# Attention of a two-block kernel's second mixer, computed by pairs of heads instead of head by head

## The chip, the cores and the metric

The kernel runs on one core of a Trainium2 chip. The core has a matrix engine (TensorE, PE in the profile, with its weight loads shown apart as PEld), a vector engine (VectorE, DVE), a scalar engine (ScalarE, ACT), GpSimd (POOL), and SyncE (SP), whose queue issues the transfers from the device's main memory. Each engine works through its own list of instructions in order; they meet through semaphores. SBUF is the on-chip memory, PSUM the accumulators into which TensorE writes; both have 128 partitions. The metric is the device time of one execution in microseconds (us).

## The reference, cut to what matters

Two transformer blocks of two layers each run one after the other on 256 tokens of width 1024. The second block's layer has a modulated norm, a mixer, and a gated feed-forward. Its mixer has three attention branches over the same 256 tokens, whose outputs are multiplied by branch weights, gated and summed:

```python
o_na = neighborhood_attention(qa, ka, va, na_rpb)        # 4 heads of 64, bias and window mask
o_mla = blocked_attention(q_full, k_full, v_b, 96**-0.5) # 4 heads, keys of 96, values of 64
o_gqa = blocked_attention(q_c, k_c, v_c, 64**-0.5)       # 8 query heads of 64 on 2 key/value heads
merged = (sigmoid(ga) * (o_na @ w_br_na) + sigmoid(gb) * (o_mla @ w_br_mla)
          + sigmoid(gc) * (o_gqa @ w_br_gqa))
x = x + g_m * (merged @ w_out)

s = einsum('bqkgd,bskd->bkgqs', qi, k) * scale           # in each dense head
p = softmax(s, axis=-1)
o = einsum('bkgqs,bskd->bqkgd', p, v)
```

All is float32. That makes 16 heads a layer and 32 in the kernel, each with 256 queries and 256 keys.

## The kernel before

All weights stream through SBUF once. A large product is done in three: both factors are split into a high part that TensorE takes at its fast rate (the type fp32r in the profile) and a low part, and the three products high x high, high x low and low x high are accumulated. ScalarE casts the high parts and VectorE subtracts for the low ones, for the weights too. The big products of a stage (projections, gates, branch weights, output) are the "main" products and write the PSUM tiles `A`. The small work of the attention runs in "lanes": Python generators that emit a step and then say, with `yield`, how many microseconds of main work should pass before their next step. The framework's scheduler then makes one fixed order for each engine out of this. On TensorE a lane's products stay behind the main product that was emitted before them (`pe_order`).

`attn` is one head. It makes the scores of two query tiles of 128 in one PSUM tile `B` (two float32 products of 256 columns, with 64 or 96 partitions of contraction), adds the bias in the four neighbourhood heads, takes the row maximum on VectorE, the exponential with row sums on ScalarE, transposes the unnormalised weights `P` by four transposes through a PSUM tile `T` (line 180 is every transpose), copies them to SBUF, and multiplies them with the values: four products with 128 queries as rows and 64 columns. VectorE scales the output by the reciprocal sums. When both heads of a pair are done, two more transposes turn the 128 output columns around, and the split pair (`ona`, `ogq`, `oml`) feeds the branch weights.

The heads are dealt to three lanes. `mix2` emits them beside the projection of keys and values, the gates and the low-rank expansions, and waits with `wait(na)`, `wait(gq)`, `wait(ml)` ahead of the three branches. Line 168 is every matrix product, lines 183, 196, 198 and 201 are VectorE's helpers, 204 the general ScalarE activation, 212 a cast and 327 the weights' cast. The tile names have one letter: `s` is a 4 KB buffer (weights, large tiles, `S4` of them), `m` one of 2 KB (13 of them), `sm` a small one, `uH` and `uL` the split input, `A`, `B`, `T` PSUM.

Ahead of the attention the mixer projects the grouped queries and normalises them (`q_post`, `gqa_norm`: a reduction on VectorE, the power -1/2 on GpSimd, then scaling and rotary embedding on VectorE, then four transposes) and prepares the low-rank query (`low_rank`, two transposes in `gain_T`), while `gemmA` makes the neighbourhood queries and keys on TensorE.

## Time and profile before

| | |
|---|---|
| time, median of 3 runs (lowest, highest) | 1990.44 us (1988.87, 1992.04) |
| span of the profiled execution, first to last instruction | 1986.1 us |
| TensorE products, busy and share of the span | 1943.7 us, 98% |
| VectorE | 1483.7 us, 75% |
| ScalarE | 1045.7 us, 53% |
| GpSimd | 100.3 us, 5% |
| HBM read | 461.58 MB, 233 GB/s over the span |
| second mixer's attention, layer 1 and layer 2 | 1212 to 1325 us, 1616 to 1730 us of the span |

The span is 4.3 us below the median of the runs; the profiled execution's own time is not listed apart, so the span plus these 4.3 us stands for it. "Busy" of TensorE counts from a product's start to its modelled end, and products overlap in the array: a high share says that it seldom stands idle, and what a product costs is read from the distance between starts.

### The profile page before, as it was taken

How to read it: one execution, taken by the hardware profiler on the slowest of the kernel's cores; microseconds unless marked ns; L12 is line 12 of the kernel's file. 1: busy time of each engine (PE TensorE's matmuls, PEld its weight loads, DVE VectorE, ACT ScalarE, POOL GpSimd, SP SyncE). 2: the span in 40 equal slices, each digit the busy share in tenths (PEclk: the TensorE clock that was granted, in tenths of full speed). 3: DMA queues.
4: the chain of work that ended last, by engine and by line, in shares of the span. 5: the costliest groups of instructions: out<-in, count | busy, mean ns of one | idle time of the engine just before them, and what ended most of it. 6: DMA issues, size and time to landing. Idle time of an engine off the chain costs nothing.

```text
span 1986.1 us, 27421 instructions
## 1 busy us (share of the span) xinstructions
PE 1943.7 (98%) x9640; PEld 1615.8 (81%) x9640; DVE 1483.7 (75%) x2045; ACT 1045.7 (53%) x1964; POOL 100.3 (5%) x164
## 2 busy tenths in 40 slices
PE   7999999999999999999999989999999999999998
PEld 5788798888888888998888878787888887878886
DVE  6878879787878878787778767568878775688552
ACT  3545566654545444476554445654644465547441
POOL 0000000000000000000100012000000020000000
PEclk9999999999999999999999999999999999999999
DMA  9989795478877897764598856357889663577650
GB/s 331 352 283 317 238 330 161 149 253 297 301 253 273 295 308 247 248 218 149 171 307 298 278 130 172 113 184 260 281 303 308 203 173 116 191 242 226 194 170 27
DMA packets 273770, 464.45 MB, mean 234 GB/s; under 512 B 30400, under 2 KB 178496, under 8 KB 273504
## 3 DMA queue, kind: packets, MB, share of 16 engines
q1 hardware_dynamic: 273632, 462.71, 71.1%
q8 instruction: 75, 1.23, 0.2%
q14 instruction: 63, 0.52, 0.1%
HBM read 461.58 MB, written 1.05 MB: 233 GB/s over the span
## 4 chain that ended last, share of the span: by engine, by line
PE 80%; issue 10%; DMA 4%; DVE 3%; ACT 1%; POOL 1%; SPq 0%; DVEq 0%; POOLq 0%; ACTq 0%
PE A L168 51%; PE B L168 24%; PE T L180 4%; DMA s<-in_ada_w 1%; DVE s L183 1%; DMA s<-in_ffn_wu 1%; DVE s L201 1%; DVE m L183 1%; DMA s<-in_w_in 1%; PE T L168 0%; ACT m L204 0%; DMA h<-in_x 0%; DMA m<-in_na_rpb 0%; ACT s L327 0%; DMA s<-in_final_norm 0%
## 5 line engine op out<-in xcount | busy, mean ns | idle before, releaser
L168 PE MATMUL A<-s,uH 128*128 128x512 f32 (+1 forms) x3008 | 952.2, 397 | 4.1 <-ACT uH L212 1.4
L183 DVE TENSOR_TENSOR s<-s,s 128x1024 fp32r<-128x1024 f32 (+3 forms) x647 | 756.7, 1183 | 157.2 <-ACT s L327 147.0
L327 ACT CAST s<-s 128x1024 fp32r<-128x1024 f32 (+1 forms) x618 | 626.9, 1044 | 55.0 <-PE A L168 20.0
L168 PEld LDWEIGHTS A<-s,uH 128*128 128x128 f32 x3008 | 553.3, 189 | 117.7 <-issue 4.6
L168 PE MATMUL A<-s,uL 128*128 128x512 f32 (+1 forms) x1504 | 588.2, 392 | 0.0
L168 PE MATMUL B<-s,m 128*128 128x512 f32 (+2 forms) x1696 | 405.1, 386 | 0.8 <-ACT m L212 0.7
L168 PEld LDWEIGHTS B<-s,m 128*128 128x128 f32 x1696 | 310.0, 189 | 62.4 <-ACT m L212 1.7
L168 PEld LDWEIGHTS A<-s,uL 128*128 128x128 f32 x1504 | 283.1, 188 | 59.9 <-DVE uL L183 1.0
L201 DVE SCALAR_TENSOR_TENSOR s<-s,sc,s 128x1024 f32<-128x1024 f32 x240 | 306.6, 1277 | 14.7 <-DMA s<-in_ada_w 14.4
L204 ACT ACTIVATE m<-A 128x256 f32<-128x256 f32 x128 | 49.2, 384 | 230.9 <-PE A L168 230.8
L212 ACT CAST m<-T 128x256 fp32r<-128x256 f32 x140 | 51.8, 372 | 158.1 <-PE T L180 157.6
L168 PE MATMUL A<-uH,s 128*128 128x256 f32 (+1 forms) x672 | 126.5, 284 | 0.0
L183 DVE TENSOR_TENSOR m<-m,A 128x256 f32<-128x256 f32 x128 | 53.2, 416 | 89.4 <-ACT m L204 89.1
L168 PE MATMUL B<-s,s 128*128 128x512 f32 (+3 forms) x432 | 104.1, 384 | 1.8 <-DVE s L201 1.3
L168 PEld LDWEIGHTS A<-uH,s 128*128 128x128 f32 (+1 forms) x672 | 104.5, 186 | 1.1
L180 PE MATMUL T<-ident,m 128*128 128x128 f32 (+1 forms) x520 | 91.4, 273 | 8.6 <-DVE m L183 5.1
L180 PEld LDWEIGHTS T<-ident,m 128*128 128x128 f32 (+1 forms) x520 | 67.8, 140 | 36.2 <-DVE m L183 7.7
L168 PE MATMUL A<-uL,s 128*128 128x256 f32 (+1 forms) x336 | 95.2, 283 | 0.0
L168 PEld LDWEIGHTS B<-s,s 128*128 128x128 f32 (+1 forms) x432 | 78.4, 188 | 17.2 <-DVE s L201 2.2
L183 DVE TENSOR_TENSOR m<-T,m 128x256 fp32r<-128x256 f32 x140 | 58.3, 419 | 45.5 <-ACT m L212 45.2
L510 POOL MEMSET s<- 128x1024 f32 x30 | 28.8, 959 | 1041.0 <-PE A L168 351.2
L204 ACT ACTIVATE m<-h 128x512 f32<-128x512 f32 x48 | 30.3, 631 | 92.1 <-DVE h L183 84.3
(177 smaller groups left out, 1473.7 us busy)
## 6 DMA issues: line engine op xcount, KB each, us to landing
s<-in_ada_w SPq DMA_DIRECT2D x224, 512.0 KB
s<-in_w_in SPq DMA_DIRECT2D x152, 512.0 KB
s<-in_ffn_wg SPq DMA_DIRECT2D x176, 256.0 KB
s<-in_ffn_wu SPq DMA_DIRECT2D x176, 256.0 KB
s<-in_ffn_wd SPq DMA_DIRECT2D x88, 512.0 KB
s<-in_ffn_w_gate_up SPq DMA_DIRECT2D x176, 256.0 KB
s<-in_ffn_w_down SPq DMA_DIRECT2D x44, 512.0 KB
s<-in_w_out SPq DMA_DIRECT2D x40, 512.0 KB
```

Of the source, the lines that this page charges most:

```text
L168: self.last = self.nc.tensor.matmul(out, l, r, start=start, stop=stop, skip_group_check=True)
L180: self.nc.tensor.transpose(out, in_, self.ident[:p, :p])
L183: self.nc.vector.tensor_tensor(o, x, y, op=op)
L201: self.nc.vector.scalar_tensor_tensor(o, x, s, y, op0=op0, op1=op1)
L204: return self.nc.scalar.activation(o, x, f, **kw)
L212: self.nc.scalar.copy(H, x)
L327: self.nc.scalar.copy(H[:, :n], raw[:, :n])
L510: self.nc.gpsimd.memset(accs[i], 0.0)
```

## The change

`attn` now takes two heads. Their scores go to two PSUM tiles, alternating: first query tile of one head, first of the other, second of the one, second of the other. In the neighbourhood and the grouped-query pairs the two heads' queries and keys lie on partitions 0 to 63 and 64 to 127, so that these products name two row halves of the array. One max tile, sum tile and reciprocal of four columns serves both heads. `P` is normalised by VectorE in SBUF before it is transposed. The values are now the stationary side, 64 columns, and the transposed `P` the moving one, 256 columns: the output comes out transposed, one head on partitions 0 to 63 and the other on 64 to 127 of one PSUM tile, and is split directly. The scaling of the outputs and the two output transposes of each pair are gone. The grouped-query heads are paired across their two key/value heads, for which the rows of `w_br_gqa` are reordered before the launch. Two lanes take the place of three. The bias tables are all emitted before the first scores, with shorter pauses. There are 37 instead of 35 `s` buffers and 16 instead of 13 `m` buffers, with a smaller scratch area for dynamic transfers. Comments were removed, which moves line numbers.

```diff
-    S4 = 35
+    S4 = 37
...
-        return self.t(shape, "m2", 13, dt)
+        return self.t(shape, "m2", 16, dt)
...
-        self.spawn([self.na_bias(l, i, bias[i]) for i in range(2)], 6.0)
+        bias_lane = self.spawn([self.na_bias(l, i, bias[i]) for i in range(2)], 6.0)
...
-        na, pn, pg, pm = [], {}, {}, {}
-        for h in range(4):
-            r = slice((h % 2) * 64, (h % 2) * 64 + 64)
-            na.append(self.attn(qaT[r, h // 2], kaT[r, h // 2], 64.0 ** -0.5,
-                                lambda kt, h=h: va[:, kt, h * 64:h * 64 + 64], h, ona, pn, bias[h // 2][:, h % 2]))
-        lanes = [self.spawn(na[0:2], 0.95), self.spawn(na[2:4], 2.5), self.spawn([], 4.0)]
+        na = []
+        for g in range(2):
+            hs = []
+            for h in (g * 2, g * 2 + 1):
+                r = slice((h % 2) * 64, (h % 2) * 64 + 64)
+                hs.append((qaT[r, g], kaT[r, g], lambda kt, h=h: va[:, kt, h * 64:h * 64 + 64], bias[g][:, h % 2]))
+            na.append(self.attn(hs, 64.0 ** -0.5, ona[0][:, g], ona[1][:, g]))
+        self.drain_inner(bias_lane)
+        lanes = [self.spawn(na[0:1], 0.95), self.spawn(na[1:2], 3.5)]
...
         gq = []
         for i in range(4):
+            hs = []
             for kv in range(2):
-                h = kv * 4 + i
                 r = slice(kv * 64, kv * 64 + 64)
-                gq.append(self.attn(qgT[r, i], kgT[r], 64.0 ** -0.5, lambda kt, r=r: vd[:, kt, r], h, ogq, pg, None))
+                hs.append((qgT[r, i], kgT[r], lambda kt, r=r: vd[:, kt, r], None))
+            gq.append(self.attn(hs, 64.0 ** -0.5, ogq[0][:, i], ogq[1][:, i]))
...
-        for i in range(8):
-            lanes[(2, 0, 1)[i % 3]].gens.append(gq[i])
+        for i in range(4):
+            lanes[i % 2].gens.append(gq[i])
...
         ml = []
-        for h in range(4):
-            ml.append(self.attn(qmT[:96, h], kmT[:96, h], 96.0 ** -0.5, lambda kt, h=h: vb[:, kt, h], h, oml, pm, None))
+        for g in range(2):
+            hs = [(qmT[:96, h], kmT[:96, h], lambda kt, h=h: vb[:, kt, h], None) for h in (g * 2, g * 2 + 1)]
+            ml.append(self.attn(hs, 96.0 ** -0.5, oml[0][:, g], oml[1][:, g]))
...
-        for i in range(4):
-            lanes[(1, 2, 0, 1)[i]].gens.append(ml[i])
+        for i in range(2):
+            lanes[i].gens.append(ml[i])
...
-            yield 6.0
+            yield 4.0
...
-    def attn(self, q, k, scale, vf, h, dst, pairs, bias):
+    def attn(self, heads, scale, H, L):
         nc = self.nc
-        b = self.pB()
+        bs = [self.pB() for _ in heads]
         for tt in range(2):
-            self.mm(b[:, tt * 256:tt * 256 + 256], q[:, tt * 128:tt * 128 + 128], k, tt == 0, tt == 1)
-        src = b
-        yield 0.9
-        if bias is not None:
-            src = self.m2([128, 512])
-            self.stt(src, b, scale, bias, ALU.mult, ALU.add)
+            for b, (q, k, _, _) in zip(bs, heads):
+                self.mm(b[:, tt * 256:tt * 256 + 256], q[:, tt * 128:tt * 128 + 128], k, tt == 0, tt == 1)
+        yield 1.2
+        bias = heads[0][3] is not None
+        mx = self.sm([128, 4])
+        srcs = []
+        for i, (b, hd) in enumerate(zip(bs, heads)):
+            src = b
+            if bias:
+                src = self.m2([128, 512])
+                self.stt(src, b, scale, hd[3], ALU.mult, ALU.add)
+            nc.vector.reduce_max(mx[:, 2 * i:2 * i + 2], src[:, :].rearrange("p (t k) -> p t k", t=2), axis=AX.X)
+            srcs.append(src)
+        if bias:
             scale = 1.0
-        mx = self.sm([128, 2])
-        nc.vector.reduce_max(mx, src[:, :].rearrange("p (t k) -> p t k", t=2), axis=AX.X)
         self.ts(mx, mx, -scale, ALU.mult)
-        yield 2.8 if bias is not None else 1.4
-        P = self.m2([128, 512])
-        sm = self.sm([128, 2])
-        for tt in range(2):
-            c = slice(tt * 256, tt * 256 + 256)
-            self.act(P[:, c], src[:, c], AF.Exp, bias=mx[:, tt:tt + 1], scale=scale, accum_out=sm[:, tt:tt + 1])
-        rc = self.sm([128, 2])
+        yield 5.0 if bias else 2.6
+        sm = self.sm([128, 4])
+        Ps = []
+        for i, src in enumerate(srcs):
+            P = self.m2([128, 512])
+            for tt in range(2):
+                c = slice(tt * 256, tt * 256 + 256)
+                j = 2 * i + tt
+                self.act(P[:, c], src[:, c], AF.Exp, bias=mx[:, j:j + 1], scale=scale, accum_out=sm[:, j:j + 1])
+            Ps.append(P)
+        rc = self.sm([128, 4])
         nc.vector.reciprocal(rc, sm)
-        yield 6.75 if bias is not None else 5.4
-        p = self.pT()
+        for i, P in enumerate(Ps):
+            for tt in range(2):
+                c = slice(tt * 256, tt * 256 + 256)
+                self.ts(P[:, c], P[:, c], rc[:, 2 * i + tt:2 * i + tt + 1], ALU.mult)
+        yield 8.4 if bias else 7.4
+        PTs = []
+        for P in Ps:
+            p = self.pT()
+            for kt in range(2):
+                for tt in range(2):
+                    o = kt * 256 + tt * 128
+                    self.tr(p[:, o:o + 128], P[:, tt * 256 + kt * 128:tt * 256 + kt * 128 + 128])
+            PT = self.m2([128, 512])
+            nc.scalar.copy(PT, p)
+            PTs.append(PT)
+            yield 1.75
+        o = bs[0]
         for kt in range(2):
-            for tt in range(2):
-                self.tr(p[:, kt * 256 + tt * 128:kt * 256 + tt * 128 + 128], P[:, tt * 256 + kt * 128:tt * 256 + kt * 128 + 128])
-        PT = self.m2([128, 512])
-        nc.scalar.copy(PT, p)
-        yield 1.75
-        for tt in range(2):
-            for kt in range(2):
-                o = kt * 256 + tt * 128
-                self.mm(b[:, tt * 64:tt * 64 + 64], PT[:, o:o + 128], vf(kt), tt == 0 and kt == 0, kt == 1)
+            for i, (PT, (_, _, vf, _)) in enumerate(zip(PTs, heads)):
+                self.mm(o[i * 64:i * 64 + 64, 0:256], vf(kt), PT[:, kt * 256:kt * 256 + 256], kt == 0, kt == 1)
         yield 0.75
-        if h // 2 not in pairs:
-            pairs[h // 2] = (self.m2([128, 2, 128]), [])
-        o, n = pairs[h // 2]
-        for tt in range(2):
-            self.ts(o[:, tt, (h % 2) * 64:(h % 2) * 64 + 64], b[:, tt * 64:tt * 64 + 64], rc[:, tt:tt + 1], ALU.mult)
-        n.append(h)
-        if len(n) == 2:
-            yield 1.2
-            p = self.pT()
-            for tt in range(2):
-                self.tr(p[:, tt * 128:tt * 128 + 128], o[:, tt])
-            self.split_sb(dst[0][:, h // 2], dst[1][:, h // 2], p[:, :256])
+        self.split_sb(H, L, o[:, 0:256])
...
+    w = arrays["w_br_gqa_2"].reshape(2, 2, 4, 64, D)
+    arrays["w_br_gqa_2"] = np.ascontiguousarray(w.transpose(0, 2, 1, 3, 4).reshape(2, 512, D))
...
-    nc = bacc.Bacc("TRN2", target_bir_lowering=False, num_devices=1)
+    nc = bacc.Bacc("TRN2", target_bir_lowering=False, num_devices=1, dynamic_dma_scratch_size=1024)
```

How the order on the engines moves, at three places of the first of the second block's layers. The first place is TensorE at the first neighbourhood scores, in the key/value projection (products `A`, 416 columns). Before, one head stands between main products, and the next comes three weight tiles later:

```order
L168 MATMUL A_11573<-s_2484_11354,uL_11049 128x416
L168 MATMUL B_11586<-m_2508_11427,m_2507_11426 128x256 x2
L168 MATMUL A_11573<-s_2488_11372,uH_11048 128x416
L168 MATMUL A_11573<-s_2489_11373,uH_11048 128x416
L168 MATMUL A_11573<-s_2488_11372,uL_11049 128x416
L168 MATMUL A_11573<-s_2488_11372,uH_11048 128x416
L168 MATMUL A_11573<-s_2489_11373,uH_11048 128x416
L168 MATMUL A_11573<-s_2488_11372,uL_11049 128x416
L168 MATMUL A_11573<-s_2491_11384,uH_11048 128x416
L168 MATMUL A_11573<-s_2492_11385,uH_11048 128x416
L168 MATMUL A_11573<-s_2491_11384,uL_11049 128x416
L168 MATMUL B_11609<-m_2508_11427,m_2507_11426 128x256 x2
```

In the changed kernel the two heads of a pair alternate; the two operands are tiles that hold one head on each half of their partitions:

```order
L168 MATMUL A_11574<-s_2484_11355,uL_11049 128x416
L168 MATMUL B_11587<-m_2509_11432,m_2508_11431 128x256
L168 MATMUL B_11588<-m_2509_11432,m_2508_11431 128x256
L168 MATMUL B_11587<-m_2509_11432,m_2508_11431 128x256
L168 MATMUL B_11588<-m_2509_11432,m_2508_11431 128x256
L168 MATMUL A_11574<-s_2488_11373,uH_11048 128x416
L168 MATMUL A_11574<-s_2489_11374,uH_11048 128x416
L168 MATMUL A_11574<-s_2488_11373,uL_11049 128x416
L168 MATMUL A_11574<-s_2488_11373,uH_11048 128x416
```

The second head's products moved up to the first one's, and the four are interleaved.

The second place is TensorE at the products with the values. Before, a head's four products of 64 columns (here `B_11849` and, further on, `B_11934`), a pair's two output transposes (`T_12077`) and the scores of another head (`B_12082`):

```order
L168 MATMUL B_11849<-m_2435_11153,m_2660_12026 128x64 x4
L168 MATMUL A_12060<-s_2570_11711,uH_11048 128x512
L168 MATMUL A_12060<-s_2571_11712,uH_11048 128x512
L168 MATMUL A_12060<-s_2570_11711,uL_11049 128x512
L180 MATMUL T_12077<-ident_68,m_2601_11819 128x128 x2
L168 MATMUL B_12082<-m_2434_11152,s_2433_11151 128x256 x2
L168 MATMUL B_11934<-m_2436_11154,m_2662_12040 128x64 x4
```

In the changed kernel, the transposes of a head's `P` (`T_11880`), a pair's four products with the values (`B_11587`, 64 partitions by 256 queries, the two heads alternating) and a pair's scores:

```order
L180 MATMUL T_11880<-ident_68,m_2593_11774 128x128 x4
L168 MATMUL A_11917<-s_2562_11686,m_2527_11571 128x512
L168 MATMUL A_11917<-s_2563_11687,m_2527_11571 128x512
L168 MATMUL A_11917<-s_2562_11686,m_2528_11572 128x512
L168 MATMUL B_11587<-m_2607_11844,m_2435_11153 64x256
L168 MATMUL B_11587<-m_2615_11872,m_2435_11153 64x256
L168 MATMUL B_11587<-m_2607_11844,m_2435_11153 64x256
L168 MATMUL B_11587<-m_2615_11872,m_2435_11153 64x256
L168 MATMUL B_11931<-m_2434_11152,s_2433_11151 128x256
L168 MATMUL B_11932<-m_2434_11152,s_2433_11151 128x256
L168 MATMUL B_11931<-m_2434_11152,s_2433_11151 128x256
L168 MATMUL B_11932<-m_2434_11152,s_2433_11151 128x256
```

Half as many products stand there, each four times as wide, and the output transposes are gone. Over the whole list 96 of 9272 products go: 64 with the values and 32 output transposes.

The third place is ahead of the attention, in `gemmA`. Before, TensorE meets the four transposes of the normalised queries (`T_11470`) and the two of the low-rank query (`T_11482`) together, after 16 products of the second half, `A_11496`:

```order
L168 MATMUL A_11496<-uL_11049,s_2470_11305 128x256
L168 MATMUL A_11496<-uH_11048,s_2471_11306 128x256
L168 MATMUL A_11496<-uH_11048,s_2470_11305 128x256
L180 MATMUL T_11470<-ident_68,m_2495_11392 128x128 x4
L180 MATMUL T_11482<-ident_68,m_2506_11424 128x128 x2
L168 MATMUL A_11496<-uL_11049,s_2470_11305 128x256
L168 MATMUL A_11496<-uH_11048,s_2471_11306 128x256
L168 MATMUL A_11496<-uH_11048,s_2475_11330 128x256
```

In the changed kernel the four (`T_11476`) stand at the end of the first half, 16 products earlier, and the two (`T_11488`) 21 products behind them:

```order
L168 MATMUL A_11433<-uL_11049,s_2475_11330 128x256
L168 MATMUL A_11433<-uH_11048,s_2476_11331 128x256
L180 MATMUL T_11476<-ident_68,m_2496_11398 128x128 x4
L168 MATMUL A_11502<-uH_11048,s_2460_11268 128x256
L168 MATMUL A_11502<-uL_11049,s_2460_11268 128x256
L168 MATMUL A_11502<-uH_11048,s_2461_11269 128x256
```

And on VectorE the work that these transposes wait for, from the reduction of the second query tile on. Before (`s` of 832 columns is the low part of a weight; `m_2494` to `m_2495` is the scaling and the rotary embedding, `m_2506` the low-rank scaling):

```order
L1378 TENSOR_REDUCE sm_11341<-m_2479_11339 128x8
L183 TENSOR_TENSOR s_2439_11157<-m_2473_11312,ctab_88 128x512
L183 TENSOR_TENSOR s_2489_11373<-s_2469_11296,s_2488_11372 128x832
L183 TENSOR_TENSOR s_2492_11385<-s_2472_11309,s_2491_11384 128x832
L183 TENSOR_TENSOR m_2494_11390<-s_2478_11337,sm_11345 128x512
L183 TENSOR_TENSOR s_2499_11409<-s_2477_11334,s_2498_11408 128x832
L183 TENSOR_TENSOR m_2496_11393<-m_2494_11390,g_2430_11135 128x512
L183 TENSOR_TENSOR m_2497_11395<-m_2494_11390,g_2430_11135 128x8x16 x4
L183 TENSOR_TENSOR m_2495_11392<-m_2496_11393,m_2497_11395 128x2x4x64
L196 TENSOR_SCALAR m_2506_11424<-s_2501_11414,sm_11422 128x256
```

In the changed kernel (`m_2495` to `m_2496`, then `m_2507`):

```order
L1378 TENSOR_REDUCE sm_11341<-m_2479_11339 128x8
L183 TENSOR_TENSOR m_2495_11396<-s_2478_11337,sm_11345 128x512
L183 TENSOR_TENSOR s_2489_11374<-s_2470_11301,s_2488_11373 128x832
L183 TENSOR_TENSOR m_2497_11399<-m_2495_11396,g_2430_11135 128x512
L183 TENSOR_TENSOR s_2493_11391<-s_2473_11314,s_2492_11390 128x832
L183 TENSOR_TENSOR m_2498_11401<-m_2495_11396,g_2430_11135 128x8x16 x4
L183 TENSOR_TENSOR m_2496_11398<-m_2497_11399,m_2498_11401 128x2x4x64
L183 TENSOR_TENSOR s_2500_11414<-s_2477_11334,s_2499_11413 128x832
L183 TENSOR_TENSOR s_2440_11158<-m_2491_11379,ctab_88 128x512
L183 TENSOR_TENSOR s_2516_11535<-s_2486_11359,s_2515_11534 128x1024
L196 TENSOR_SCALAR m_2507_11429<-s_2502_11419,sm_11427 128x256
```

Two weights' low parts moved from ahead of the scaling to behind its start, so that two instead of one now stand inside the chain that ends in the transposed tile.

## Rows read from the trace of the kernel before

**Rows 1.** The page: span, engines' busy time, TensorE's granted clock in 40 slices.

```profile
span 1986.1 us, 27421 instructions
PE 1943.7 (98%) x9640; PEld 1615.8 (81%) x9640; DVE 1483.7 (75%) x2045; ACT 1045.7 (53%) x1964; POOL 100.3 (5%) x164
...
PEclk9999999999999999999999999999999999999999
```

**Rows 2.** Windows over the attention of both layers: busy (instructions), clock, DMA share, GB/s.

```profile
1212.00:1325.00 113.00, 112.31 (x595) 91.71 (x594) 72.84 (x164) 68.50 (x162) 10.41 (x18) 1.00 0.48 151
1616.00:1730.00 114.00, 113.31 (x596) 92.54 (x595) 73.94 (x164) 68.06 (x150) 8.33 (x13) 1.00 0.48 154
```

**Rows 3.** Timeline of TensorE, scores: start, duration, merged rows, idle before.

```profile
1213.72 1.13 PE L168 MATMUL B<-m,m 64*128 64x256 f32 x4
1214.78 0.65 PE L168 MATMUL A<-s,uH 128*128 128x416 f32 x2
...
1302.51 1.03 PE L168 MATMUL B<-s,s 96*128 96x256 f32 x4
1303.37 0.38 PE L180 MATMUL T<-ident,m 128*128 128x128 f32 x2
1303.59 1.03 PE L168 MATMUL B<-s,s 96*128 96x256 f32 x4
```

**Rows 4.** Timeline of TensorE, a head's products with the values, then transposes.

```profile
1253.14 1.00 PE L168 MATMUL B<-m,m 128*128 128x64 f32 x8
1253.98 1.05 PE L180 MATMUL T<-ident,m 128*128 128x128 f32 x8
```

**Rows 5.** Groups of TensorE by shape, 1212 to 1352 us: count, busy, mean ns, idle.

```profile
L168 PE MATMUL B<-m,m 128*128 128x64 f32 x128 | 16.2, 270 | 0.0
L168 PE MATMUL B<-m,s 64*128 64x256 f32 x32 | 9.0, 402 | 0.0
L168 PE MATMUL B<-m,m 64*128 64x256 f32 x16 | 4.5, 402 | 0.0
L168 PE MATMUL B<-s,s 96*128 96x256 f32 x16 | 4.1, 379 | 0.0
L180 PE MATMUL T<-ident,m 128*96 128x128 f32 x16 | 2.6, 273 | 0.7 <-ACT s L1537 0.7
```

**Rows 6.** Timeline of TensorE at the transposes ahead of the attention, both layers.

```profile
1204.13 0.28 PE L168 MATMUL A<-uL,s 128*128 128x256 f32 x1
1204.25 0.40 PE L168 MATMUL A<-uH,s 128*128 128x256 f32 x2
1205.72 0.66 PE L180 MATMUL T<-ident,m 128*128 128x128 f32 x4 [1.07 <-DVE m L183]
1208.40 0.41 PE L180 MATMUL T<-ident,m 128*128 128x128 f32 x2 [2.02 <-DVE m L196]
...
1612.27 0.88 PE L180 MATMUL T<-ident,m 128*128 128x128 f32 x6 [1.07 <-DVE m L183]
```

**Rows 7.** Timeline of VectorE at the same place, first layer.

```profile
1201.91 0.69 DVE L183 TENSOR_TENSOR m<-s,sm 128x512 f32<-128x512 f32 x1 [1.83 <-POOL sm L219]
1202.52 1.02 DVE L183 TENSOR_TENSOR s<-s,s 128x832 fp32r<-128x832 f32 x1
1203.45 1.49 DVE L183 TENSOR_TENSOR m<-m,g 128x512 f32<-128x512 f32 x5
1207.90 0.35 DVE L196 TENSOR_SCALAR m<-s,sm 128x256 f32<-128x256 f32 x1 [2.23 <-POOL sm L219]
```

**Rows 8.** Groups of VectorE and of ScalarE by shape, 1212 to 1352 us.

```profile
L1669 DVE TENSOR_REDUCE sm<-B 128x2 f32<-128x512 f32 x12 | 8.2, 685 | 1.6 <-PE B L168 1.5
L196 DVE TENSOR_SCALAR m<-B,sm 128x64 f32<-128x64 f32 x32 | 8.0, 276 | 12.7 <-PE B L168 12.6
...
L204 ACT ACTIVATE m<-B,sm 128x256 f32<-128x256 f32 x24 | 11.2, 473 | 8.2 <-DVE sm L196 8.1
L204 ACT ACTIVATION_READ_ACCUMULATOR m<-B,sm 128x1 f32 x24 | 4.8, 201 | 0.0
```

## The prediction

> **What bounds the kernel now.** [...] Then the windows over the two stretches of attention: TensorE is busy for 112.3 of 113 and 113.3 of 114 us, VectorE for about 73, ScalarE for 68, the transfers take 0.48 of the DMA engines' time [rows 2]. So nothing but the length of TensorE's own list sets the end here. What a product costs is then not its listed mean, which contains the pipeline's depth, but the distance between starts, so I read the timeline. Last come the few waits of TensorE around the mixer [rows 5, 6].

> **What the changed products cost now.** In these rows one float32 product shows as two records, so a head's two score products are four. With 96 partitions of contraction four records take 1303.37 - 1302.51 = 0.86 us, 0.215 each. With 64 partitions the same four take 1214.78 - 1213.72 = 1.06 us: entering a row half and leaving it costs 0.20 us more [rows 3]. A head's products with the values, eight records of 64 columns, take 1253.98 - 1253.14 = 0.84 us [rows 4]. Two output transposes take 1303.59 - 1303.37 = 0.22 us [rows 3]. The counts, 48 records with 64 partitions, 16 with 96 and 128 with the values in the first layer, are 12, 4 and 16 heads [rows 5], which is 6 pairs with row halves and 8 pairs in all. Over both layers: 12 pairs' scores at 2 x 1.06 = 2.12 us and 16 pairs' values with output transposes at 2 x 0.84 + 0.22 = 1.90 us, 25.4 + 30.4 = 55.8 us. The scores of the 96-partition pairs and the transposes of `P` keep their cost.

> **What they cost afterwards.** Scores of a pair are again eight records of 256 columns, and the values become eight records of 256 columns too (64 columns of weights are taken to cost as much as 128, so that the width of the moving side counts). One after the other that is 8 x 0.215 = 1.72 us, with 0.20 for entering and leaving 1.92. So with no overlap of halves the change is worth 12 x (1.92 - 2.12) + 16 x (1.92 - 1.90) = -2.1 us: all of the gain hangs on two halves running at once, which no row of before shows, since a head's records all lie on one half. The bounds: if the halves overlap wholly, four lengths, 0.86 + 0.20 = 1.06 us, 12 x (-1.06) + 16 x (-0.84) = -26.1 us; if each change of half inside a group costs half of that 0.20, three times 0.10 on top of 1.92, then 2.22 us, 12 x 0.10 + 16 x 0.32 = +6.3 us.

> Between them I go by the order. A float32 product's two records are neighbours and share a half, and TensorE starts in order, so the list is A A B B A A B B: only the second record of one head can run beside the first of the other. That is five lengths, 5 x 0.215 + 0.20 = 1.28 us. If the weights of the other half are loaded only once the record before has started, each change shows about 0.1 us, half of the entering and leaving, on three changes more: 1.075 + 0.30 + 0.20, about 1.6 us. I take the middle, 1.44 us: scores 12 x (1.44 - 2.12) = -8.2, values 16 x (1.44 - 1.90) = -7.4, together -15.5 us; with 1.28 it is -20.0, with 1.6 it is -11.0.

> [...]

> **The waits ahead of the attention.** TensorE waits there for VectorE's rotary result, 1.07 us in both layers, and in the first for the low-rank scaling, 2.02 us [rows 6]. The order moves the four transposes 16 products up, 16 x 0.12 = 1.9 us (the starts 1204.13 and 1204.25 stand 0.12 apart [rows 6]), and puts one more weight subtraction, 1203.45 - 1202.52 = 0.93 us from its start to the next [rows 7], into the chain that starts when GpSimd's power comes. VectorE idled 1.83 us before that chain, so its start does not move. The wait becomes 1.07 + 1.9 + 0.93 = 3.9 us. In the first layer the low-rank wait goes, since 2.5 us of products now stand between; 3.9 against 3.1 is +0.8. In the second only the 1.07 goes against it, +2.9. On the other side, the wait of 0.7 us in each layer for ScalarE's copy of the 96-row transposes [rows 5] should go, because these groups are now 9 main products apart: -1.4. Together +2.3 us.

> **What is hidden.** VectorE scales `P` with four instructions of 256 columns, 0.35 us each by the nearest row [rows 7], in place of four of 64 columns at 0.28 [rows 8]: +0.3 us a pair beside 40 idle us a stretch. The scaling now stands in front of the transposes of `P`. For a pair the path from its scores is two maxima of 0.69, four exponentials with their sums of 0.47 + 0.20 [rows 8], four scalings, two of which the first head needs, about 5.1 us in all, 1.4 more with the bias; the new order leaves 13 to 17 us of main products there (counted, at 0.12 us for 256 columns). If less than 5 were left, each missing microsecond would stop TensorE, and the main products behind it. The bias loads move up on SP by a few places and add no bytes; the extra buffers take away waits that TensorE does not show. The reordered weight rows are the same bytes.

> **Sum.** -15.5 + 2.3 = -13.2 us on the profiled execution, 1986.1 + 4.3 = 1990.4; that equals the median of the runs, so 1977 us.

> **Rivals.** (a) No overlap at all: -2.1 + 2.3, 1990.6 us, no change. For it: the trace has no overlapped pair. Against it: weight loads fill 1615.8 us beside products that fill 98% [rows 1], so work on one record does run beside another now. (b) Slower: a change of half drains inside the groups, 0.10 us each time, from [rows 3]; +6.3 + 2.3 gives 1999 us. It decides as soon as a group of eight records takes over 2.0 us. (c) Rows overlap, columns don't. Both column halves use all row groups, and in [rows 4] eight narrow records take 0.84 us, 0.105 each where 0.215 x 64/256 = 0.054 would move them, so there the loads set the pace one by one. Then the values cost 1.92 us: -8.2 + 0.3 + 2.3 = -5.6, 1984.8 us. [...] (d) Whole overlap, -26.1 + 2.3: 1966.6 us. (e) Pairs late: two lanes of pairs hold both PSUM tiles longer, and where the transposes of `P` come before VectorE's scaling, 0.8 us for each of 16 pairs cancels the gain; the 13 to 17 us speak against it.

> **How the numbers follow.** Chances: forecast (partial overlap of both, 1972 to 1982) 0.47, (a) 0.21, (b) 0.10, (c) 0.12, (d) 0.07, (e) 0.03. A difference within 0.2%, 4.0 us, is what this measurement can't tell from none. Faster are the forecast, (c) and (d), 0.66; same is (a), 0.21; slower (b) and (e), 0.13. The range leaves out (b), (e) and the far end of (d): 1966 to 1992 us.

> **What would show it.** In the new profile a pair's eight score records with 64 partitions should take 1.3 to 1.6 us up to the next main product, and the eight with the values (64 columns of weights, 256 moving) as much, with records of the other half starting before 0.215 us are over. The transposes ahead of the attention should wait about 4 us in each layer. VectorE's 256-column scaling should show no wait of TensorE behind it. I am wrong if a group takes 1.9 us or more, if starts stay 0.215 us apart, or if TensorE stands waiting inside the attention.

## The result

The changed kernel takes 1962.47 us (median of 4 runs, 1960.75 to 1964.0) against 1990.12 us for the kernel before (median of 4 runs), a ratio of 0.986 with a 95% interval of 0.9846 to 0.9874. That is 27.7 us less. The forecast was 1977 us with a range of 1966 to 1992: the sign was right, the gain was twice the forecast one, and the time lies below the range. The rival that comes nearest is (d), whole overlap, 1966.6 us, which had a chance of 0.07.

The page of the changed kernel, lines that answer to [rows 1]:

```profile
span 1962.2 us, 27021 instructions
PE 1918.2 (98%) x9480; PEld 1584.8 (81%) x9480; DVE 1482.7 (76%) x2013; ACT 1042.8 (53%) x1964; POOL 96.1 (5%) x164
...
PEclk9999999999999999999999999999999999999999
```

TensorE is still the bound with 98%, and its busy time fell by 1943.7 - 1918.2 = 25.5 us; VectorE's and ScalarE's stayed. This execution took 1964.0 us with a span of 1962.2, so 1.8 us lie outside the span. By that the profiled execution of before (span 1986.1) took some 1987.9 us, 2.2 below the median; the 4.3 us that the prediction took for it were too many, and the two traces differ by 23.9 us only.

Where the time went is best read from main products that both traces have. The table gives the start of the same product in each (us from the span's start) and how far it moved:

| place | before | after | moved |
|---|---|---|---|
| end of the first block | 1116.1 | 1117.9 | +1.8 |
| layer 1, first projection in the attention | 1221.8 | 1223.9 | +2.1 |
| layer 1, last main products of the mixer | 1342.4 | 1331.7 | -10.7 |
| layer 1, feed-forward | 1383.1 | 1370.7 | -12.4 |
| layer 2, first projection in the attention | 1628.9 | 1619.3 | -9.6 |
| layer 2, last main products of the mixer | 1746.9 | 1724.3 | -22.6 |
| layer 2, feed-forward | 1786.0 | 1762.0 | -23.9 |

The first 1.8 us arise within the first 60 us of the kernel, where nothing was changed; over all traces of this document the same product there starts between 60.2 and 62.4 us. The rest is three pieces, both layers together: +3.1 us ahead of the attention (0.3 and 2.8), -25.8 in it (12.8 and 13.0), -3.0 at the hand-over to the feed-forward (1.7 and 1.3). They add up to -25.7 us. The medians differ by 27.7 us, and 25.7 lies inside the interval of that difference (25.1 to 30.6 us).

**The attention.** The timeline of TensorE in the changed kernel, a pair's products with the values, a pair's scores, and what follows:

```profile
1241.94 1.08 PE L168 MATMUL B<-m,m 128*64 128x256 f32 x8
1242.95 1.14 PE L168 MATMUL B<-m,s 64*128 64x256 f32 x8
1244.02 0.33 PE L180 MATMUL T<-ident,m 128*128 128x128 f32 x1
```

From start to start, eight records with the values take 1242.95 - 1241.94 = 1.01 us and eight score records 1244.02 - 1242.95 = 1.07 us. A single head's four score records took 1.06 us before [rows 3]: the second head costs nothing. The same timeline cut to 0.06 us shows why, and record by record the eight starts are four pairs, 6 or 7 ns apart within a pair, with 0.32 us from the first pair to the second and 0.215 us between the others:

```profile
1242.95 0.49 PE L168 MATMUL B<-m,s 64*128 64x256 f32 x2
```

One pair in each layer does not come out like this:

```profile
1246.37 1.08 PE L168 MATMUL B<-m,m 128*64 128x256 f32 x8
1247.75 0.73 PE L168 MATMUL A<-s,uH 128*128 128x512 f32 x2 [0.30 <-DVE m L1525]
...
1248.64 1.50 PE L168 MATMUL B<-m,s 64*128 64x256 f32 x8
1250.07 0.50 PE L168 MATMUL A<-s,uH 128*128 128x512 f32 x1
```

Its scores take 1250.07 - 1248.64 = 1.43 us, because the second head's first product carries a wait of its own (for VectorE's line 183, which is still reading its PSUM tile) and starts 0.37 us late. In the list these two heads stand one behind the other. The second row shows one of the few waits left inside the attention, 0.30 us for a copy by VectorE; the others are 0.67 us in the first layer and 0.71 in the second for the scaling of the low-rank keys. In the windows the attention is as full as before [rows 2]:

```profile
1214.00:1317.00 103.00, 101.92 (x535) 78.94 (x535) 73.27 (x152) 67.98 (x165) 9.87 (x18) 1.00 0.52 168
1606.00:1709.00 103.00, 102.07 (x536) 79.24 (x536) 74.03 (x152) 65.68 (x149) 7.60 (x13) 1.00 0.51 167
```

**Ahead of the attention.** All engines at the place of [rows 6, 7], first layer:

```profile
1203.67 0.28 PE L168 MATMUL A<-uH,s 128*128 128x256 f32 x1
...
1204.60 0.69 DVE L183 TENSOR_TENSOR m<-m,m 128x512 f32<-128x512 f32 x1
...
1205.35 0.66 PE L180 MATMUL T<-ident,m 128*128 128x128 f32 x4 [1.40 <-DVE m L183]
...
1206.04 0.59 ACT L1396 COPY s<-T 128x512 f32<-128x512 f32 x1 [8.72 <-PE T L180]
...
1206.53 0.59 ACT L1412 COPY s<-A 128x512 f32<-128x512 f32 x1
...
1207.17 0.58 PE L168 MATMUL A<-uH,s 128*128 128x256 f32 x1 [1.16 <-ACT s L1412]
1207.55 0.42 PE L168 MATMUL A<-uL,s 128*128 128x256 f32 x1
```

The four transposes wait 1.40 us for the rotary result. The next main product waits 1.16 us more: it needs a PSUM tile that ScalarE's line 1412 empties, and that copy stands in ScalarE's list behind line 1396, which waits for these transposes. The wait of 2.02 us for the low-rank scaling is gone in this layer (in the second one of 0.60 us is new). Then the granted clock falls; the window over the next 3 us has it at 0.50, the lower of the two levels in these traces (1.00 and 0.50), after 3.5 us in which TensorE did little but four transposes:

```profile
1207.00:1210.00 3.00, 2.83 (x13) 2.83 (x14) 1.24 (x2) 3.00 (x7) 1.88 (x6) 0.50 0.76 208
```

Starts stand 0.21 us apart there in place of 0.12, some 13 x 0.09 = 1.2 us lost. In the second layer the same two waits (1.38 and 1.16 us) leave the clock at its upper level, 1.00 over 1598 to 1608 us. Across this place alone the same main products moved by 0.85 us in the first layer and by 2.5 in the second. The table's 0.3 for the first layer also holds what lies between 1116 and 1202 us, where the kernel before had the clock at 0.50 over 1166 to 1169 us of its trace and the changed kernel did not.

The chain behind the 1.40 us did not start where it did before. VectorE and GpSimd from the reduction on, first the kernel before, then the changed one:

```profile
1196.93 0.68 DVE L1378 TENSOR_REDUCE sm<-m 128x8 f32<-128x512 f32 x1
1198.13 1.95 DVE L183 TENSOR_TENSOR s<-s,s 128x832 fp32r<-128x832 f32 x2
...
1197.70 2.44 POOL L217 TENSOR_SCALAR sm<-sm 128x8 f32<-128x8 f32 x1 [10.28 <-DVE sm L1378]
```

```profile
1197.85 0.69 DVE L1378 TENSOR_REDUCE sm<-m 128x8 f32<-128x512 f32 x1
1198.63 0.20 POOL L217 TENSOR_SCALAR sm<-sm 128x8 f32<-128x8 f32 x1 [10.29 <-DVE sm L1378]
...
1200.59 0.69 DVE L183 TENSOR_TENSOR m<-s,sm 128x512 f32<-128x512 f32 x1 [2.05 <-POOL sm L219]
```

Before, VectorE went on with other work behind the reduction, the two low parts among it that the change moves, and GpSimd's first instruction took 2.44 us and ended 0.06 us after that work did. In the changed kernel VectorE stood idle there and the instruction took 0.20 us (GpSimd's times are rough). From the reduction's end to the scaling it is 4.30 us before [rows 7] and 2.05 after. In the second layer the instruction takes 2.44 and 0.20 us too. No run changes this alone.

**The hand-over.** First the kernel before, then the changed one, first layer, TensorE at the first products behind the mixer:

```profile
1361.52 1.20 PE L168 MATMUL B<-s,s 128*128 128x512 f32 x4 [0.25 <-ACT s L204]
1363.89 0.50 PE L168 MATMUL B<-s,s 128*128 128x512 f32 x1 [1.17 <-DVE s L201]
```

```profile
1350.27 1.96 PE L168 MATMUL B<-s,s 128*128 128x512 f32 x6 [0.25 <-ACT s L204]
```

A wait of 1.17 us for VectorE's line 201 is gone. No step of the prediction looked there.

### The profile page after: what moved, and what is told of

Its sections match the earlier page's. It is cut to its first block, busy times and chain, and to the rows that moved or that the text cites. A ratio compares the mean times of both kernels' runs of the same rounds, so it can differ in the third digit from the quotient of the medians.

```text
span 1962.2 us, 27021 instructions
## 1 busy us (share of the span) xinstructions
PE 1918.2 (98%) x9480; PEld 1584.8 (81%) x9480; DVE 1482.7 (76%) x2013; ACT 1042.8 (53%) x1964; POOL 96.1 (5%) x164
## 3 DMA queue, kind: packets, MB, share of 16 engines
q8 instruction: 74, 1.21, 0.2%
## 4 chain that ended last, share of the span: by engine, by line
PE 77%; issue 11%; DVE 5%; DMA 4%; ACT 1%; POOL 1%; SPq 0%; DVEq 0%; POOLq 0%; ACTq 0%
PE A L168 50%; PE B L168 22%; PE T L180 4%; DVE s L183 2%; DMA s<-in_ada_w 2%; DVE m L183 1%; DVE s L201 1%; DMA s<-in_w_in 1%; DMA s<-in_ffn_wg 1%; ACT m L204 0%; DMA ctab<-in_ctab 0%; PE T L168 0%; ACT s L327 0%; DMA h<-in_x 0%; POOL sm L219 0%
## 5 line engine op out<-in xcount | busy, mean ns | idle before, releaser
L201 DVE SCALAR_TENSOR_TENSOR s<-s,sc,s 128x1024 f32<-128x1024 f32 x240 | 307.2, 1280 | 12.5 <-DMA s<-in_ada_w 12.3
L180 PE MATMUL T<-ident,m 128*128 128x128 f32 (+1 forms) x488 | 84.5, 274 | 8.0 <-DVE m L183 5.9
L180 PEld LDWEIGHTS T<-ident,m 128*128 128x128 f32 (+1 forms) x488 | 62.8, 139 | 35.0 <-DVE m L183 9.0
```

Source lines behind the costliest of these rows:

```text
L180: self.nc.tensor.transpose(out, in_, self.ident[:p, :p])
L201: self.nc.vector.scalar_tensor_tensor(o, x, s, y, op0=op0, op1=op1)
```

## The experiments

The theory after the result: a head's records wait in a queue of the half that they use, and records of the other half pass them; two halves run at once whatever the alternation. The rivals: only neighbours in the list overlap; or the gain comes from fewer instructions, from lanes or from buffers.

**Head after head.** In scores and values the two loops change places, so that one head's products are all issued before the other's:

```diff
-        for tt in range(2):
-            for b, (q, k, _, _) in zip(bs, heads):
+        for b, (q, k, _, _) in zip(bs, heads):
+            for tt in range(2):
...
-        for kt in range(2):
-            for i, (PT, (_, _, vf, _)) in enumerate(zip(PTs, heads)):
+        for i, (PT, (_, _, vf, _)) in enumerate(zip(PTs, heads)):
+            for kt in range(2):
```

> Of the changed kernel only the order inside a group is changed: all products of one head, then all of the other (records A A A A B B B B), for the scores and for the values. Theory (each half of the array has its own queue, and a record of the other half may start while earlier ones of the first half still wait): the groups stay at 1.06 and 1.01 us, the time at 1962 us within 3. Rival (starts keep the order of the list, and only the alternation lets neighbours overlap): one overlapped length of eight, 7 x 0.215 + 0.20 = 1.7 us a group, 28 groups x 0.65 = +18 us, 1980 us.

Measured: 1962.61 us, ratio 0.9868 (0.9853 to 0.9882). Its timeline, whole groups and then the first 0.07 us of the second one:

```profile
1239.82 1.09 PE L168 MATMUL B<-m,m 128*64 128x256 f32 x8
1240.84 1.14 PE L168 MATMUL B<-m,s 64*128 64x256 f32 x8
1241.91 0.55 PE L180 MATMUL T<-ident,m 128*128 128x128 f32 x3
```

```profile
1240.84 0.49 PE L168 MATMUL B<-m,s 64*128 64x256 f32 x2
```

The groups keep 1.02 and 1.07 us. Two records start at once although four of the first head stand in the list ahead of the second head's first; the only trace of the order is that starts within a pair lie 13 ns apart instead of 7. The rival of neighbours falls.

**How far ahead.** The score products of each head, head after head, are issued twice and four times (the loop `for tt in (0, 1) * 2`, then `* 4`); the added work repeats what is there.

> Head after head as in the first experiment, and each head's score products are issued twice (eight records of one head, then eight of the other; the second set writes the same values again). Theory (a half's records wait in a queue of their own while the other half starts): eight lengths and the entering and leaving, 8 x 0.215 + 0.20 = 1.92 us a group with 64 partitions, starts in pairs as before. Rival (only about four records are held, which the first experiment needed): the other half starts when the fifth record of the first has started, 4 x 0.215 = 0.86 us later, 2.8 us a group. With no overlap 16 x 0.215 + 0.20 = 3.6 us.

> The same with each head's score products issued four times (sixteen records of one head, then sixteen of the other). Theory with a deep queue: 16 x 0.215 + 0.20 = 3.64 us a group. Rival (a queue of some depth below sixteen): the second head's first record starts late by 0.215 us for each record beyond that depth, up to 32 x 0.215 + 0.20 = 7.1 us a group.

Measured: 1990.15 and 2044.63 us (one run each; what follows is read from the traces). The first group of the twofold run, its first 0.05 us, and the 0.10 us in which the second head appears:

```profile
1213.51 2.96 PE L168 MATMUL B<-m,m 64*128 64x256 f32 x16
1216.40 0.45 PE L168 MATMUL A<-s,uH 128*128 128x416 f32 x1
```

```profile
1213.51 0.48 PE L168 MATMUL B<-m,m 64*128 64x256 f32 x1
...
1214.26 0.70 PE L168 MATMUL B<-m,m 64*128 64x256 f32 x3
```

The first group of the fourfold run:

```profile
1214.12 6.42 PE L168 MATMUL B<-m,m 64*128 64x256 f32 x32
1220.47 0.64 PE L168 MATMUL A<-s,uH 128*128 128x416 f32 x2
```

The group takes 1216.40 - 1213.51 = 2.89 us, not 1.92. Only one record starts at the beginning. In the later cut there are three, the fourth of the first head (1214.26) and two that start 6 ns apart at 1214.48: the fifth of the first head and the first of the second. In the fourfold run this first pair of starts is at the 13th of 16, and a group takes 1220.47 - 1214.12 = 6.35 us. So with 4, 8 and 16 records of one head in front, the other head begins beside the 1st, the 5th and the 13th: as soon as three records of the first half are left waiting. The rival of the twofold run (2.8 us) was right, and by these starts the queue is short: the kernel's four records a head, one running and three waiting, are just what it holds. The eight and sixteen were run on row halves only, column halves with four.

**One part alone.** The loops stand as in the first experiment, for the scores only (in the first run) or for the values only (in the second), and a pause inside the loop puts some three main products between the heads:

```diff
-        yield 1.2
+            yield 0.6
```

```diff
-        yield 0.75
+            yield 0.7
```

> Of the changed kernel only the scores are changed: the second head's products come three main products behind the first head's. Theory (the gain is two row halves at once): each head's four records alone take 1.06 us, so the twelve pairs with 64 partitions cost 12 x 1.06 = 12.7 us more, less 0.7 for the two pairs that overlap only in part now: about 1974.5 us. Rival (the gain comes from fewer instructions, lanes or buffers): 1962 us within 3.

> Of the changed kernel only the products with the values are changed: in 14 of the 16 pairs the second head's come three main products behind the first head's. Theory (two column halves at once): a head's four records alone take as long as the group now, 1.01 us, so 14 x 1.01 = +14 us, about 1976.5 us. Rival (column halves do not overlap; the narrower weights alone make the products short): no change, 1962 us within 3.

Measured: 1976.31 us (ratio 0.9936, 0.9922 to 0.9951) and 1981.04 us (0.9958, 0.9942 to 0.9975): 13.8 and 18.6 us above the changed kernel, where some 12 and 14 were expected. The first timeline is of the scores apart, the second of the values apart:

```profile
1212.96 0.35 PE L168 MATMUL A<-s,uL 128*128 128x416 f32 x1
1213.24 1.13 PE L168 MATMUL B<-m,m 64*128 64x256 f32 x4
1214.30 0.65 PE L168 MATMUL A<-s,uH 128*128 128x416 f32 x2
1214.79 0.35 PE L168 MATMUL A<-s,uL 128*128 128x416 f32 x1
```

```profile
1266.15 0.40 PE L168 MATMUL A<-s,uL 128*128 128x512 f32 x1
1266.39 0.62 PE L168 MATMUL A<-s,uH 128*128 128x512 f32 x2
1266.85 0.40 PE L168 MATMUL A<-s,uL 128*128 128x512 f32 x1
1267.17 1.08 PE L168 MATMUL B<-m,m 128*64 128x256 f32 x4
1268.18 0.73 PE L168 MATMUL A<-s,uH 128*128 128x512 f32 x2
1268.75 0.39 PE L168 MATMUL A<-s,uL 128*128 128x512 f32 x1
```

One head alone takes 1.06 and 1.01 us, as long as two heads together. Column halves overlap as wholly as row halves.

Both runs cost more than expected, because a group costs more than the time from its first start to the next product's. In the second timeline a main product is followed after 0.24 us (1266.15 to 1266.39) and two after 0.46 (1266.39 to 1266.85), but the one just ahead of the group after 0.32 and the two just behind it after 0.57 (1268.18 to 1268.75). These 0.09 and 0.11 us outside make 1.21 us of a group with column halves; in the first timeline 0.28 and 0.49 us, where 0.19 and 0.38 are usual in that stretch, make 1.26 of one with row halves. The main products show it directly: in the first run those of the key/value projection fall back by 2.51 us against the changed kernel over their two pairs of scores. By these prices the scores cost 10 x 1.26 - 0.7 = 11.9 us, since one pair in each layer kept its eight records together, and the values 14 x 1.21 + 2 x 1.26 - 0.5 = 18.9 us, since one pair of scores in each layer fell apart too; 0.7 and 0.5 us are what the late pair gains. Between the same main products of the traces the attention of both layers is 12.5 and 17.1 us longer than in the changed kernel; the rest up to 13.8 and 18.6 lies outside the attention.

**Both apart.** The two edits together.

> The pair structure without the overlap: five of six score pairs with 64 partitions and seven of eight pairs' products with the values in each layer have their second head three main products behind the first. Theory: 2 x (5 x 1.06 + 7 x 1.01) = +24.7 us on the changed kernel, with 2 to 5 us more for late steps as in the two runs that did one part each: 1987 to 1992 us, which is about the kernel before. Rival (the two parts share a cost, so that their sum counts something twice): clearly less than +25, under 1984 us.

Measured: 1990.91 us, ratio 1.0005 (0.9996 to 1.0014). Without the overlap the pair structure is worth nothing, though it has fewer instructions, other lanes and other buffers. The edits take two things away, however: of the 1.26 us that a second group of scores costs, 0.86 us are four lengths that no longer run beside others, and 0.40 us a second entering and leaving. Between the same main products the attention is 28.2 us longer than in the changed kernel, 2.4 longer than in the kernel before; the 3.0 us at the hand-over stay.

**Buffers alone.** The kernel before with 37 and 16 tiles and the smaller scratch area.

> The kernel before with the buffers of the change alone (37 and 16 tiles, the smaller scratch area). Theory: TensorE's list is the same and it waits for no buffer, so 1990 us within 3. Rival (a part of the gain comes from buffers): 1985 us or less.

Measured: 1988.33 us, ratio 0.9993 (0.9984 to 1.0003): no difference that can be told from none.

**The waits ahead of the attention.** First the transposes of the queries alone are moved, then those of the low-rank keys as well:

```diff
-                yield 5.6
+                yield 9.0 if pair else 5.6
```

```diff
-            self.later(4.5, lambda: self.gain_T(c, H, L, g, n // 128))
+            self.later(4.5 if n > 128 else 6.0, lambda: self.gain_T(c, H, L, g, n // 128))
```

> The changed kernel with the transposes of the normalised grouped queries ordered 3.4 us of main work later (nothing else). Theory (the order of the change put them ahead of VectorE's chain, and ScalarE's copy of them ahead of the copy that frees a PSUM tile): the waits of 1.40 and 1.16 us in each layer go, with the shorter ones ahead of the first query tile's, 0.5 and 0.8: 3 to 6 us less, 1957 to 1959 us. Rival (the low-rank transposes wait in their place, 2.02 us as in the kernel before): 1961 to 1963 us.

> As the run before, and the transposes of the low-rank keys and values 1.5 us later as well. Theory: the wait of 0.67 us for VectorE's low-rank scaling inside the attention goes in each layer and the scores whose second PSUM tile came late (1.42 in place of 1.06 us) stay as they are: 1 to 1.5 us less than the run before. Rival (the products of the low-rank expansion wait longer for their split input instead): the same time as the run before.

Measured: 1965.88 us (0.9883, 0.9866 to 0.9899) and 1966.65 us (0.989, 0.9875 to 0.9905), 3.4 and 4.2 us above the changed kernel (the first interval still touches that kernel's). TensorE in the first of them:

```profile
1206.97 0.69 PE L180 MATMUL T<-ident,m 128*128 128x128 f32 x2 [5.56 <-DVE m L196]
```

The rival was right and stronger than forecast: with the four gone, the two low-rank transposes came earlier and waited 5.56 us. In the first layer GpSimd has rotary tables (lines 1360 and 1364) in its list ahead of the power that they need; in the second, without these there, they still waited 3.92 us. In both layers the granted clock is at 0.50 for a part of this stretch too (in the first run over 1204 to 1210 and 1600 to 1606 us), so not all of the loss is waiting. In the second run these two waits stay (5.57 and 3.95 us), and the one for the low-rank keys only moved to other transposes (0.61 and 0.59 us in each layer). So both sets were moved, the four tied to their place in the list of main products:

```diff
-                yield 5.6
+                yield 9.5 if pair else 5.6
...
+                with self.pe_order():
...
-            self.later(4.5, lambda: self.gain_T(c, H, L, g, n // 128))
+            self.later(12.0 if n > 128 else 4.5, lambda: self.gain_T(c, H, L, g, n // 128))
```

> The changed kernel with the transposes of the normalised queries tied to a place 24 main products later, and those of the low-rank query 39 later (past the products of the next projection, where GpSimd's power and VectorE's scaling should be done). Theory: neither set waits; of the 1.40, 1.16 and 0.6 us of waits in each layer nothing or under 0.5 us is left: 3 to 6 us less than the changed kernel, 1957 to 1960 us. Rival (VectorE itself stands waiting for the low-rank power, so the weights' low parts come late and TensorE waits for them instead): 1961 to 1964 us.

Measured: 1952.5 us, ratio 0.9812 (0.9799 to 0.9826), faster than both kernels. The groups of TensorE from 1195 to 1212 us, first of this run, and then of the changed kernel from 1195 to 1214 us:

```profile
L168 PE MATMUL A<-uH,s 128*128 128x256 f32 x64 | 12.0, 285 | 0.0
...
L180 PE MATMUL T<-ident,m 128*128 128x128 f32 x11 | 1.7, 272 | 0.0
```

```profile
L168 PE MATMUL A<-uH,s 128*128 128x256 f32 x61 | 12.8, 306 | 1.2 <-ACT s L1412 1.2
...
L180 PE MATMUL T<-ident,m 128*128 128x128 f32 x6 | 1.0, 282 | 1.4 <-DVE m L183 1.4
```

No wait is left at this place in either layer, and the products have the mean again that they have where the granted clock is 1.00 (285 in place of 306 ns). The same main products moved by 5.2 us in the first layer and 4.9 in the second. That is more than the 3 to 6 us expected for both: ahead of the four transposes and behind them the changed kernel's starts stand 1.68 and 1.82 us apart, in this run 0.12 and 0.36, which is 3.0 us and not the idle 2.56; the waits of 0.55 and 0.82 us at the transposes of the first query tile are gone as well; and in the first layer so are the 1.2 us of the lower clock.

## Why the prediction was wrong

**The step that failed** is the one between the bounds: "TensorE starts in order, so the list is A A B B A A B B: only the second record of one head can run beside the first of the other", which gave groups of 1.28 to 1.6 us and 1.44 as the value taken. That order was assumed: no row of before has two halves in one group. By the starts of the runs with 4, 8 and 16 records in front (the other head beside the 1st, the 5th and the 13th), a record that waits for its own half does not hold up one for the other, up to three waiting. The groups measure 1.06 and 1.01 us, four lengths and one entering and leaving. With these the scores are worth 10 x 1.06 + 2 x 1.43 - 25.4 = -11.9 us in place of -8.2, the values 16 x 1.01 - 30.4 = -14.2 in place of -7.4: together -26.1 us instead of -15.5, the lower bound that the prediction had worked out itself.

Starts do not keep the order of the list here: in the run head after head the second head's first record starts 13 ns after the first of the four that precede it, ahead of the other three. Nor do column halves wait for each other: in the changed kernel their products, which use all rows, are loaded and start in pairs as those of the row halves do, 6 or 7 ns apart. Of the ends nothing is shown, since the profile models them.

**What was mis-sized without harm.** The 0.20 us for entering and leaving are only what lies inside a group; with the neighbours it is 1.26 - 0.86 = 0.40 us for row halves and 1.21 - 0.86 = 0.35 for column halves. With these the scores are worth 12 x 1.26 - 24 x 1.26 + 0.7 = -14.4 us and the values 16 x 1.21 - 30.4 = -11.0, together -25.4: fewer groups for the scores and dearer ones for the values nearly cancel, which is luck.

**What was right.** TensorE's list sets the time, and nearly the whole gain hangs on overlap: with both parts apart it is gone (1990.91 us). That rival (a) said 1990.6 for no overlap is in part luck, since it paid the entering and leaving once for both heads and that run pays it twice. The price is paid once a group and not at each change of half, so rival (b) falls. Rival (c) falls with the column halves. `P` scaled ahead of its transposes caused no wait, as forecast, and rival (e) left only the one late PSUM tile in each layer, 0.37 us. The buffers add nothing.

**The waits ahead** came to 0.85 + 2.5 = +3.4 us for 0.8 + 2.9 = +3.7 forecast (3.9 - 1.07 is 2.8), but by two errors that cancel. The forecast wait of 3.9 us was 1.40, because the step "so its start does not move" failed: from the reduction to the scaling it took 2.25 us less, as GpSimd's instruction was shorter. And 1.16 us behind ScalarE's list, in the first layer with the lower clock after them, and 0.60 for the low-rank scaling in the second were not in the sum. The wait of 0.7 us for line 1537 went in both layers (-1.4), as forecast; the others in the attention took its place.

**What the sum lacked:** -3.0 us at the hand-over, where VectorE's line 201 is no longer late. The attention itself: -25.4 to -26.1, with -1.4 for line 1537 and 0.67, 0.71 and 0.30 back, makes -25.1 to -25.8; -25.8 was measured. What made VectorE earlier at the hand-over was not tried by itself; it is not the overlap, since the gain stays with both parts apart.

The range ended at 1966 because whole overlap had 0.07. No row of before spoke against it; the order of starts that was held against it was an assumption, not a reading. The signs of being wrong that the prediction named all lay on the slow side.

## What to carry to other kernels

Two small products on different halves of TensorE's array cost here as much as one, for row halves (1.06 us a group with one head or with two) and for column halves (1.01) alike, if at most four records (two float32 products) of one half stand in the list ahead of the other's and neither half's first product carries a late wait of its own (more than four were tried on row halves only). Keep such products together: each group pays its 0.35 to 0.40 us anew, about half of it at its neighbours, where the time from its first start to the next product's does not show it. Where no trace shows whether two things overlap, give whole overlap a real chance and let the range reach it. After such a gain look at the small transposes ahead of the stage: where two of them hang on a slow chain, move both, since moving one let the other wait in its place (5.56 us).

## What was not expected of the hardware

Whether the clock falls differs between places with the same rows. The same pair of waits (1.36 to 1.40 us and 1.16, with four transposes between) stands in both layers of five traces: the changed kernel, head after head, scores apart, values apart, both apart. About the end of the second wait the granted clock falls to its lower level (0.50) in five of these ten places (the first layer of the changed kernel and of the values apart, the second of the scores apart, both of head after head) and stays at its upper level (1.00) in the other five. The kernel before waited 1.07 and 2.02 us in its first layer [rows 6] with the clock at 1.00 over 1200 to 1212 us; with other buffers and the same waits (1.09 and 2.02) the clock is at 0.50 over 1209 to 1212 us. So a microsecond or two between two traces here need not come from a change. The digits of [rows 1] and of the page above hide such a fall, since each is a mean over 50 us.
